# First tiles of a fused encoder block: small weights ahead of x, x's first tile in halves, some first weights through ScalarE's queue

## The chip, the cores and the metric

One NeuronCore of a Trainium2 chip. The metric is the device time of one execution in microseconds (us). A core has five engines that run beside each other: TensorE (PE in the rows; its weight loads are PEld), VectorE (DVE), ScalarE (ACT), GpSimd (POOL) and SyncE (SP), and 16 DMA engines that move data between the device's memory and the on-chip memory. SP, ACT and POOL can issue transfers.

## What is computed

One layer of a hybrid encoder trunk on x of 512 positions by 1024 channels, in float32. Cut to what stands at its start:

```
hn   = rms_norm(x, g_mix_pre)          # x * rsqrt(mean(x*x) + eps) * g
proj = hn @ w_in                       # 1024 -> 8192 columns
z_sgu, z_conv, z_pool, z_gate = split(proj)
br_b = conformer_conv(z_conv, ...) @ w_conv_out     # GLU, causal depthwise conv, layer norm, swish
...
h = x + rms_norm((gates * (br_a, br_b, br_c)).sum() @ w_out, g_mix_post)
h = h + rms_norm(swiglu(rms_norm(h, g_ffn_pre)), g_ffn_post)
out = h + sigmoid(h @ w_ple_gate) * (p @ w_ple)
```

## The kernel before, in words

Channels lie on the 128 partitions, the 512 positions along the free axis, so x is eight k-tiles of 128 channels by 512 positions. To keep float32 accuracy on TensorE, every operand is split into a high part (rounded) and a low part (the remainder), and each product is done three times: high by high, high by low, low by high (`mm3`, and `passes` in line 458). ScalarE makes a high part by a copy that rounds, VectorE the low part by a subtraction (`split`, line 177).

The order of the work at the start is written out by hand under `order()` (lines 459 to 518), which pins each instruction behind the one traced before it on its engine. The first products (`first_product`, lines 451 to 455) are six column blocks of 128 of the projection, the first three pairs of the conformer branch. They run with k outermost: for each k-tile of x, 3 passes by 6 blocks, 18 products of 128 by 512, into six accumulators (`banks`, line 449). x enters these products scaled by `g_mix_pre` alone; the factor of the norm, `x_inv`, comes later in `glu`. `x_high(k)` (line 388, ScalarE) scales and rounds a tile of x, `x_low(k)` (line 391, VectorE) makes its low part, `w_split(k)` (line 395) splits the 768 columns of weights of k-tile k. For k-tile 0 the weights come in two cuts (`first_cuts`, line 135): columns 0 to 255, blocks 0 and 1, whose high part VectorE makes (line 462), and columns 256 to 767, the other four blocks. Between, ScalarE squares x's tiles and VectorE sums the squares (`x_square`, `x_sums`); the two halves of the sums go through TensorE against a constant matrix (`channel_mean`, line 495, tile `ps_stat`), between the second and the third pass of k-tile 3.

The transfers are issued in lines 138 to 149: the vector of per-channel scales (`vec`) on ScalarE's queue, all else on SP's, in this order: x's tile 0, the two cuts of weights of k-tile 0, x's tile 1, the weights of k-tile 1, x's tiles 2 and 3, the weights of k-tile 2, x's tiles 4 to 7, the weights of k-tiles 3 to 7 (`X_AHEAD`, line 50, says how many tiles of x go ahead of each). A tile of x has 256 KB, a k-tile's weights 384 KB.

Before the data are there, TensorE runs a warm-up on zeros (lines 163 to 167): eight products of 512 columns and one of 256. VectorE fills the constant matrix and the zeros first; ScalarE makes a copy of one column (line 162), ahead of which stands the load of its activation table.

Of the kernel before, what the change touches and what calls it, by code (L numbers as in the profile page):

```python
# [8 lines left out]
F32 = mybir.dt.float32  # L9
F32R = mybir.dt.float32r  # L10
BF16 = mybir.dt.bfloat16
I32 = mybir.dt.int32
AF = mybir.ActivationFunctionType
# [3 lines left out]
P = 128  # L17
T = 512
H = 256
D = 1024  # L20
KT = D // P
NB = T // P
# [8 lines left out]
HALVES = (slice(0, H), slice(H, T))  # L31
FULL = slice(0, T)
# [8 lines left out]
N_RAW = 3  # L41
N_FIRST = 2 * N_RAW * P

N_WARM = 8

TAPS = (4, 3, 5, 3, 5)
TAPS_U = 4
# [2 lines left out]
X_AHEAD = (1, 2, 4, 8, 8, 8, 8, 8)  # L50

DMA_K = 5
STAT_K, STAT_A, STAT_H = 3, 1, 7

K_HALF = 4
# [36 lines left out]
def hybrid_block(  # L92
# [7 lines left out]
    nc = tc.nc  # L100
    order = InOrder(tc)
    dve, act_e = order.engine(nc.vector), order.engine(nc.scalar)
    pe_order = InOrder(tc)
    pe = pe_order.engine(order.engine(nc.tensor))

    const = ctx.enter_context(tc.tile_pool(name="const", bufs=1))
# [13 lines left out]
    def slot(tag, name, dt=F32R, shape=(2, T)):  # L120
        return act.tile([P, *shape], dt, tag=tag, name=name, bufs=6 if tag == "tm" else 8)
# [9 lines left out]
    x_all = wide_tile("x_all")  # L131
    first_all = wide.tile([P, KT * T], F32, tag="wide", name="first_all")
    first_raw = []

    def first_cuts(k):
        return ((0, 2 * P), (2 * P, N_FIRST)) if k == 0 else ((0, N_FIRST),)

    nc.scalar.dma_start(out=vec[:, :N_VEC], in_=vecs[:, :N_VEC])
    x_ahead = 0
    for k in range(KT):  # L140
        if k < 5:
            first_raw.append(first_all[:, k * N_FIRST:(k + 1) * N_FIRST])
        else:
            first_raw.append(slot("hn", "first_raw", F32, (D,))[:, :N_FIRST])
        while x_ahead < X_AHEAD[k]:
            nc.sync.dma_start(out=x_all[:, x_ahead], in_=xT[:, x_ahead])
            x_ahead += 1
        for c0, c1 in first_cuts(k):
            nc.sync.dma_start(out=first_raw[k][:, c0:c1], in_=w_first[k][:, c0:c1])

    def col(name, k):
        i = VECS.index(name) * KT + k
        return vec[:, i:i + 1]

    def tap(k, j):
        i = N_VEC + k * WIDTH + j
        return vec[:, i:i + 1]

    mean_mat = const.tile([P, P], F32R, name="mean_mat")
    dve.memset(mean_mat.bitcast(F32), 1.0 / D)  # L160
    warm = const.tile([P, 1], F32, name="warm")
    act_e.copy(warm, mean_mat.bitcast(F32)[:, :1])
    warm_up = const.tile([P, T], BF16, name="warm_up")
    dve.memset(warm_up, 0.0)
    ps = psum.tile([P, T], F32, tag="pst", name="ps_warm", bufs=1)
    for n in N_WARM * (T,) + (H,):
        pe.matmul(ps[:, :n], lhsT=warm_up[:, :P], rhs=warm_up[:, :n], start=True, stop=True)
    ident = const.tile([P, P], F32, name="ident")
    make_identity(nc, ident)
    cnt_i = const.tile([P, WINDOWS[-1]], I32, name="cnt_i")  # L170
# [61 lines left out]
    def blk(w, k):  # L232
        return w[:, k * P:(k + 1) * P]
# [144 lines left out]
    xg = [slot("br", f"xg{k}") for k in range(KT)]  # L378
    x_sums = row("x_sums")
    first = []  # L380
# [4 lines left out]
            pair = [stream.tile([P, D], F32R, tag=t, name=t) for t in ("hi", "lo")]  # L385
        first.append([w[:, :N_FIRST] for w in pair])

    def x_high(k):
        act_e.activation(out=xg[k][:, 0], in_=x_all[:, k], func=AF.Copy, scale=col("g_mix_pre", k))

    def x_low(k):
        dve.scalar_tensor_tensor(out=xg[k][:, 1], in0=x_all[:, k], scalar=col("g_mix_pre", k),
                                 in1=xg[k][:, 0], op0=ALU.mult, op1=ALU.subtract)
# [55 lines left out]
    banks = [bank("ps_first") for _ in range(2 * N_RAW)]  # L449

    def first_product(k, passes, js=range(2 * N_RAW)):
        for w, a in passes:
            for j in js:
                pe.matmul(banks[j], lhsT=blk(first[k][w], j), rhs=xg[k][:, a],
                          start=k == 0 and w == a == 0, stop=k == KT - 1 and w == 1)


    passes = ((0, 0), (0, 1), (1, 0))
    with order():
        (c0, c1), cut = first_cuts(0)  # L460
        hi, lo = (w[:, c0:c1] for w in first[0])
        dve.tensor_copy(hi, first_raw[0][:, c0:c1])
        x_high(0)
        dve.tensor_tensor(out=lo, in0=first_raw[0][:, c0:c1], in1=hi, op=ALU.subtract)
        x_low(0)
        hi, lo = (w[:, slice(*cut)] for w in first[0])
        split(hi, lo, first_raw[0][:, slice(*cut)])
        first_product(0, passes, range(c1 // P))
        first_product(0, passes, range(c1 // P, 2 * N_RAW))
        x_square(0)  # L470
        x_high(1)
        w_split(1)
        x_low(1)
        x_square(1)
        x_square(2)
        first_product(1, passes)
        x_high(2)
        w_split(2)
        x_low(2)
        for k in range(3, 6):  # L480
            x_square(k)
        first_product(2, passes)
        x_high(3)
        w_split(3)
        for k in range(6, KT):
            x_square(k)
        x_low(3)
        for k in (4, 5):
            x_high(k)
            w_split(k)  # L490
            if k == 4:
                x_halves = split_sums(x_sums)
            x_low(k)
        first_product(3, passes[:2])
        ps_x = channel_mean(x_sums, x_halves)
        first_product(3, passes[2:])
        for k in range(4, KT):
            if k >= 6:
                x_high(k)
                w_split(k)  # L500
        weights.ahead(2)
        weights.split = split
        rsqrt(x_inv, ps_x, t2("rs_t"))
        x_low(6)
        x_low(7)
        low = None
        for i in range(KT):
            t = t2("nrm")
            dve.scalar_tensor_tensor(out=t, in0=x_all[:, i], scalar=col("g_mix_pre", i),
                                     in1=x_inv, op0=ALU.mult, op1=ALU.mult)  # L510
            act_e.copy(hn[i][:, 0], t)
            if low:
                low()
            low = lambda i=i, t=t: dve.tensor_tensor(out=hn[i][:, 1], in0=t, in1=hn[i][:, 0],
                                                     op=ALU.subtract)
        low()
        for k in range(4, KT):
            first_product(k, passes)
# [3 lines left out]
    for k in range(N_RAW, KT):  # L522
        pair = []
        for _ in range(2):
            ps = bank("ps_ag")
            w = weights.get()
# [137 lines left out]
    for n in range(KT + SGU_LAG):  # L664
# [7 lines left out]
        else:  # L672
            i = n - SGU_LAG
            ps = branch_tile(sgu_T, TAPS[2])
# [38 lines left out]
    for g in GROUPS:  # L713
        for n in (2 * g, 2 * g + 1):
            ps = bank("ps_z")
# [9 lines left out]
    for n in range(KT + POOL_LAG):  # L725
# [6 lines left out]
        if n >= POOL_LAG:  # L732
            i = n - POOL_LAG
            ps = branch_tile(pool_T, TAPS[4])
# [30 lines left out]
    for n in range(KT):  # L765
        ps = branch_tile(conv_T, 0)
# [67 lines left out]
    with order():  # L834
# [6 lines left out]
        for i in range(N_HALF):  # L841
            n = KT - N_HALF + i
# [9 lines left out]
        for i in range(N_HALF):  # L852
            n = KT - N_HALF + i
# [11 lines left out]
        banks = [bank("ps_f") for _ in range(2 * N_PAIR)]  # L865
# [67 lines left out]
    for n in range(KT - 2):  # L933
        ps = bank("ps_fo")
# [31 lines left out]
    with order():  # L966
        ps, ps_last = bank("ps_fo"), bank("ps_fo")
        ffn_out(ps, KT - 2, 0, weights.get(2))
        ffn_out(ps_last, KT - 1, 0, weights.get(1))
        w = weights.get(1)  # L970
        ffn_out(ps, KT - 2, 1, w)
        weights.ahead(3)
        w = weights.get(2)
# [16 lines left out]
        for n in range(KT):  # L990
            hs = FULL if n < KT - 1 else HALVES[0]
            ps = ple_product(n, w_ple_1 if n >= 4 else w_ple_0, p_w, hs,
                             (lambda: inv_rms(f_sums, f_inv)) if n == PLE_STAT else None)
# [4 lines left out]
        banks = [bank("ps_pg") for _ in range(N_LAST)]  # L998
        for k, a in enumerate(h2):

            for w, x in ((0, 0), (1, 0), (0, 1)):
                for ps, block in zip(banks, blocks):
                    pe.matmul(ps, lhsT=blk(block[w], k), rhs=a[:, x],
                              start=k == w == x == 0, stop=k == KT - 1 and x == 1)
# [81 lines left out]
```

## Time and profile before

| | us |
|---|---|
| median of 3 runs | 973.61 (973.38 to 973.9) |
| the profiled execution | 974.28 |
| its span, first to last instruction | 972.5 |
| TensorE busy in it | 966.9 |
| VectorE, ScalarE busy | 673.3, 349.9 |

The profile shows one execution, instruction by instruction; times count from the first instruction. The profiled execution took 974.28 us, of which 972.5 are the span and 1.78 lie around it; it is 0.67 us slower than the median of the unprofiled runs. A DMA issue is a short instruction on the issuing engine's sequencer; its data land later.

### The profile page before, as it was taken

The numbers are of one execution on the slowest core, as the hardware profiler recorded it, in microseconds if no ns is written. First come the engines' busy times: TensorE is split into PE (matmuls) and PEld (weight loads), VectorE is DVE, ScalarE is ACT, GpSimd is POOL, SyncE is SP. The second block draws the span as 40 slices with busy tenths as digits, with TensorE's granted clock in tenths as the row PEclk, the third lists the DMA queues.
The fourth block names the chain that finished last, engine by engine and source line by source line (L and its number), as shares of the span: only waits on it lengthen the run. The fifth ranks groups of instructions, "written<-read, shape, count | busy, mean of one in ns | idle before, by whom it ended". The sixth has DMA issues, their size and how long they took to land.

```text
span 972.5 us, 11143 instructions
## 1 busy us (share of the span) xinstructions
PE 966.9 (99%) x4429; PEld 804.4 (83%) x4429; DVE 673.3 (69%) x868; ACT 349.9 (36%) x467; POOL 70.9 (7%) x51
## 2 busy tenths in 40 slices
PE   9999999999999999999999999999999999999998
PEld 6888888888888888888888988888888888888887
DVE  6997789999988899987555787544444442223684
ACT  7622333432224432156425353323232322223451
POOL 0100004000013712130000000000000000000000
PEclk9999999999999999999999999999999999999999
DMA  8832331322322332232337203222322333334311
GB/s 291 197 109 87 110 107 66 108 87 87 109 85 78 98 108 87 94 123 87 109 97 263 74 26 105 87 97 98 99 97 89 104 82 99 99 100 144 109 66 65
DMA packets 30724, 102.72 MB, mean 106 GB/s; under 512 B 3536, under 2 KB 4048, under 8 KB 30672
## 3 DMA queue, kind: packets, MB, share of 16 engines
q1 hardware_dynamic: 29808, 99.75, 31.0%
q0 software_dynamic: 720, 2.23, 1.3%
q8 instruction: 34, 0.56, 0.2%
q14 instruction: 18, 0.15, 0.0%
q10 hardware_dynamic: 144, 0.04, 0.0%
HBM read 97.68 MB, written 2.10 MB: 103 GB/s over the span
## 4 chain that ended last, share of the span: by engine, by line
PE 99%; DMA 1%; SPq 0%; DVE 0%; ACT 0%; issue 0%; DVEq 0%
PE ps_f L79 25%; PE ps_gate L79 13%; PE ps_br L79 13%; PE ps_fo L79 12%; PE ps_nat L79 9%; PE ps_ag L79 6%; PE ps_o L79 5%; PE ps_pg L79 5%; PE ps_z L79 4%; PE ps_first L79 3%; PE ps_ple L79 1%; PE ps_pool L79 1%; DMA first_all<-in_w_first 1%; PE ps_mix L79 1%; PE ps_stat L79 0%; PE ps_tr L79 0%
## 5 line engine op out<-in xcount | busy, mean ns | idle before, releaser
L79 ACT CAST hi<-raw 128x1024 fp32r<-128x1024 f32 (+2 forms) x160 | 165.2, 1033 | 459.4 <-PE ps_br L79 82.5
L79 DVE TENSOR_TENSOR lo<-raw,hi 128x1024 fp32r<-128x1024 f32 (+2 forms) x158 | 206.9, 1310 | 110.0 <-ACT hi L79 109.7
L79 DVE SCALAR_TENSOR_TENSOR acc<-h_conv,vec,acc 128x511 f32<-128x511 f32 (+14 forms) x240 | 183.1, 763 | 5.0
L79 PE MATMUL ps_f<-hg,hi 128*128 128x512 f32 (+1 forms) x608 | 183.3, 383 | 0.0
L79 PEld LDWEIGHTS ps_f<-hg,hi 128*128 128x128 f32 x608 | 113.1, 188 | 22.4
L79 PE MATMUL ps_gate<-hn,hi 128*128 128x512 f32 x384 | 119.0, 389 | 0.0
L79 PE MATMUL ps_f<-hg,lo 128*128 128x512 f32 (+1 forms) x304 | 116.4, 383 | 0.0
L79 PE MATMUL ps_fo<-f,hi 128*128 128x512 f32 x352 | 108.3, 389 | 0.0
L79 PEld LDWEIGHTS ps_gate<-hn,hi 128*128 128x128 f32 x384 | 72.0, 188 | 15.1
L79 PE MATMUL ps_nat<-hi,hn 128*128 128x512 f32 x256 | 78.8, 389 | 0.0
L79 PEld LDWEIGHTS ps_fo<-f,hi 128*128 128x128 f32 x352 | 66.1, 188 | 13.7
L79 PE MATMUL ps_gate<-hn,lo 128*128 128x512 f32 x192 | 74.8, 389 | 0.0
L79 PE MATMUL ps_fo<-f,lo 128*128 128x512 f32 x176 | 68.5, 389 | 0.0
L79 PEld LDWEIGHTS ps_f<-hg,lo 128*128 128x128 f32 x304 | 57.1, 188 | 11.3
L79 DVE TENSOR_TENSOR f<-ps_f,h_inv 128x512 f32<-128x512 f32 x22 | 15.2, 690 | 59.3 <-PE ps_f L79 59.3
L79 PEld LDWEIGHTS ps_nat<-hi,hn 128*128 128x128 f32 x256 | 48.0, 188 | 9.9
L79 PE MATMUL ps_nat<-lo,hn 128*128 128x512 f32 x128 | 49.8, 389 | 0.0
L79 PE MATMUL ps_ag<-hn,hi 128*128 128x512 f32 x160 | 49.2, 389 | 0.0
L79 PEld LDWEIGHTS ps_gate<-hn,lo 128*128 128x128 f32 x192 | 36.0, 188 | 7.5
L79 DVE TENSOR_TENSOR silu<-ps_f,h_inv 128x512 f32<-128x512 f32 x22 | 15.2, 690 | 36.7 <-PE ps_f L79 36.6
L79 PE MATMUL ps_br<-pool,hi 128*128 128x512 f32 x128 | 39.6, 389 | 0.0
L79 PE MATMUL ps_br<-sgu,hi 128*128 128x512 f32 x128 | 39.4, 389 | 0.0
(223 smaller groups left out, 1490.6 us busy)
## 6 DMA issues: line engine op xcount, KB each, us to landing
raw<-in_w_mix SPq DMA_DIRECT2D x90, 512.0 KB, 3.2
raw<-in_w_ffn_in SPq DMA_DIRECT2D x44, 512.0 KB, 3.2
raw<-in_w_ffn_out SPq DMA_DIRECT2D x16, 448.0 KB, 3.3
raw<-in_w_ffn_out SPq DMA_DIRECT2D x8, 512.0 KB, 3.5
raw<-in_w_ple_gate SPq DMA_DIRECT2D x8, 512.0 KB, 3.9
x_all<-in_xT SPq DMA_DIRECT2D x8, 256.0 KB, 7.2
h_all<-in_xT SPq DMA_DIRECT2D x4, 512.0 KB, 5.4
out_dram<-pg SPq DMA_DIRECT2D x7, 256.0 KB, 2.0
```

Source lines behind the costliest of these rows:

```text
L79: inst = op(*args, **kw)
```

## The change: order, size and queue of the first transfers, and the order of k-tile 0

- `N_WARM` goes from 8 to 7, and the warm-up's operand is a 128 by 128 tile, filled first, that is read four times over for the 512 columns.
- SP's first transfer is the first cut of k-tile 0's weights, then x's tile 0 in two halves of 256 positions. The second cut goes on ScalarE's queue, behind the vector.
- The weights of k-tile 1 (`K_ACT`) go on ScalarE's queue as well, pinned behind the copy of one column. All other transfers keep their queue and order.
- k-tile 0: x is scaled in halves; high and low weights of blocks 0 and 1 are multiplied with the high part of each half as it comes (eight half-width products), then the other four blocks' first pass, then the passes that are left.

```
+K_ACT = 1
-N_WARM = 8
+N_WARM = 7
...
+        cuts = first_cuts(k)
+        if k == 0:
+            c0, c1 = cuts[0]
+            nc.sync.dma_start(out=first_raw[0][:, c0:c1], in_=w_first[0][:, c0:c1])
+            cuts = cuts[1:]
+            for hs in HALVES:
+                nc.sync.dma_start(out=x_all[:, 0, hs], in_=xT[:, 0, hs])
+            x_ahead = 1
+            (c0, c1), cuts = cuts[0], ()
+            nc.scalar.dma_start(out=first_raw[0][:, c0:c1], in_=w_first[0][:, c0:c1])
         while x_ahead < X_AHEAD[k]:
             nc.sync.dma_start(out=x_all[:, x_ahead], in_=xT[:, x_ahead])
             x_ahead += 1
-        for c0, c1 in first_cuts(k):
-            nc.sync.dma_start(out=first_raw[k][:, c0:c1], in_=w_first[k][:, c0:c1])
+        if k != K_ACT:
+            for c0, c1 in cuts:
+                nc.sync.dma_start(out=first_raw[k][:, c0:c1], in_=w_first[k][:, c0:c1])
...
+    warm_up = const.tile([P, P], BF16, name="warm_up")
+    dve.memset(warm_up, 0.0)
     mean_mat = const.tile([P, P], F32R, name="mean_mat")
     dve.memset(mean_mat.bitcast(F32), 1.0 / D)
     warm = const.tile([P, 1], F32, name="warm")
-    act_e.copy(warm, mean_mat.bitcast(F32)[:, :1])
-    warm_up = const.tile([P, T], BF16, name="warm_up")
-    dve.memset(warm_up, 0.0)
+    with order():
+        act_e.copy(warm, mean_mat.bitcast(F32)[:, :1])
+        tc.keep_in_program_order(nc.scalar.dma_start(out=first_raw[K_ACT], in_=w_first[K_ACT]))
     ps = psum.tile([P, T], F32, tag="pst", name="ps_warm", bufs=1)
-    for n in N_WARM * (T,) + (H,):
-        pe.matmul(ps[:, :n], lhsT=warm_up[:, :P], rhs=warm_up[:, :n], start=True, stop=True)
+    ps = ps.rearrange("p (n c) -> p n c", n=NB)
+    for n in N_WARM * (NB,) + (NB // 2,):
+        pe.matmul(ps[:, :n], lhsT=warm_up, rhs=warm_up[:, None, :].broadcast_to([P, n, P]),
+                  start=True, stop=True)
...
-    def x_high(k):
-        act_e.activation(out=xg[k][:, 0], in_=x_all[:, k], func=AF.Copy, scale=col("g_mix_pre", k))
+    def x_high(k, hs=FULL):
+        act_e.activation(out=xg[k][:, 0, hs], in_=x_all[:, k, hs], func=AF.Copy,
+                         scale=col("g_mix_pre", k))
...
         dve.tensor_copy(hi, first_raw[0][:, c0:c1])
-        x_high(0)
         dve.tensor_tensor(out=lo, in0=first_raw[0][:, c0:c1], in1=hi, op=ALU.subtract)
+        for hs in HALVES:
+            x_high(0, hs)
+
+            for w in range(2):
+                for j in range(c1 // P):
+                    pe.matmul(banks[j][:, hs], lhsT=blk(first[0][w], j), rhs=xg[0][:, 0, hs],
+                              start=hs is HALVES[0] and w == 0, stop=False)
         x_low(0)
         hi, lo = (w[:, slice(*cut)] for w in first[0])
         split(hi, lo, first_raw[0][:, slice(*cut)])
-        first_product(0, passes, range(c1 // P))
-        first_product(0, passes, range(c1 // P, 2 * N_RAW))
+        rest = range(c1 // P, 2 * N_RAW)
+        first_product(0, passes[:1], rest)
+        first_product(0, passes[1:2], range(c1 // P))
+        first_product(0, passes[1:], rest)
```

## Rows read from the trace of the kernel before

**Rows 1.** The page: busy time of each engine (us, share of the span, instructions), and the shares of the engines in the chain that ended last.

```profile
PE 966.9 (99%) x4429; PEld 804.4 (83%) x4429; DVE 673.3 (69%) x868; ACT 349.9 (36%) x467; POOL 70.9 (7%) x51
...
PE 99%; DMA 1%; SPq 0%; DVE 0%; ACT 0%; issue 0%; DVEq 0%
```

**Rows 2.** The chain of work that ended last, first 42 us: start and length in us, what.

```profile
1.65 0.42 SPq L149
...
2.12 0.43 SPq L146
...
2.59 6.85 DMA first_all<-in_w_first
...
9.46 0.84 ACT first L79
...
10.35 11.49 PE ps_first L79 x48
```

**Rows 3.** The same chain over the whole span, two long pieces: 240 full products, 60 products of 256 columns.

```profile
40.01 54.40 PE ps_ag L79 x240
...
544.84 7.19 PE ps_o L79 x60
```

**Rows 4.** The timeline of the first 9 us, all engines: start, length, engine, line, instruction, out<-in and shapes, count, and in brackets the idle time before and what ended it.

```profile
0.74 0.40 ACTq L138 DMA_DIRECT2D vec<-in_vecs  x1
...
1.00 0.27 DVE L79 MEMSET warm_up<- 128x256 uint32 x1
...
1.17 1.28 ACT L79 ACT_TABLE_LOAD   x1 [1.17 <-PEq L1074]
...
1.33 3.81 PE L79 MATMUL ps_warm<-warm_up 128*128 128x512 bf16 x9 [1.33 <-DVE warm_up L79]
...
4.19 0.72 ACT L79 ACTIVATE xg<-x_all,vec 128x512 fp32r<-128x512 f32 x1 [1.53 <-DMA vec<-in_vecs]
...
4.55 4.24 SPq L146 DMA_DIRECT2D x_all<-in_xT  x4
...
4.96 4.81 PE L79 MATMUL ps_first<-xg,first 128*128 128x512 f32 x18
```

**Rows 5.** Two weight loads of the warm-up and the one at 12.00, from TensorE's timelines; and of the tile xg the row of its full products (duration ns min/median/max, first and last start).

```profile
2.16 0.15 PEld L79 LDWEIGHTS <-warm_up 128*128 128x128 bf16 x1 [0.28 <-issue]
2.59 0.15 PEld L79 LDWEIGHTS <-warm_up 128*128 128x128 bf16 x1 [0.28 <-issue]
...
12.00 2.15 PEld L79 LDWEIGHTS ps_first<-xg,first 128*128 128x128 f32 x10 [0.43 <-DVE xg L79]
...
L79 PE MATMUL ps_first<-xg,first x101: 387/389/797, 5.0 to 29.9; 128*128 128x512 f32 x101
```

**Rows 6.** Busy time in stretches of the start: stretch, length, then busy us and instructions of PE, PEld, DVE, ACT, POOL, then the granted clock, the busy share of the 16 DMA engines and GB/s.

```profile
4.00:6.00 2.00, 2.00 (x7) 0.83 (x6) 1.59 (x4) 1.74 (x3) 0.00 (x0) 1.00 0.74 212
6.00:8.00 2.00, 2.00 (x10) 1.68 (x10) 0.39 (x1) 0.14 (x1) 0.00 (x0) 1.00 0.91 298
8.00:10.00 2.00, 1.77 (x8) 1.13 (x6) 0.00 (x0) 1.26 (x2) 0.00 (x0) 1.00 1.02 387
10.00:12.00 2.00, 1.65 (x6) 1.05 (x6) 1.67 (x3) 2.00 (x5) 0.00 (x0) 1.00 1.05 405
```

**Rows 7.** Single transfers of the start, each from a stretch that holds its issue alone: out<-in, issuing queue, count, KB, us from issue to landing. In order: x's tile 0 (issued 0.74), the first cut of weights (1.18), the second (1.65), x's tile 1 (2.12), k-tile 1's weights (2.59), k-tile 3's weights (9.46).

```profile
x_all<-in_xT SPq DMA_DIRECT2D x1, 256.0 KB, 3.2
...
first_all<-in_w_first SPq DMA_DIRECT2D x1, 128.0 KB, 3.2
...
first_all<-in_w_first SPq DMA_DIRECT2D x1, 256.0 KB, 3.3
...
x_all<-in_xT SPq DMA_DIRECT2D x1, 256.0 KB, 6.3
...
first_all<-in_w_first SPq DMA_DIRECT2D x1, 384.0 KB, 6.8
...
first_all<-in_w_first SPq DMA_DIRECT2D x1, 384.0 KB, 6.0
```

**Rows 8.** A group of ScalarE's instructions by shape, from the second half of the kernel: the same operation as the scaling of x, on 256 columns: count, busy us, mean ns of one, idle before.

```profile
L79 ACT ACTIVATE hg<-h_all,vec 128x256 fp32r<-128x256 f32 x8 | 4.1, 511 | 9.5 <-DVE h_all L79 9.5
```

**Rows 9.** What SP's queue waited for in the first 20 us: us in total, times, longest.

```profile
SPq L146 <- DMA x_all<-in_xT: 1.8, 1, 1.8
SPq L149 <- DMA first_all<-in_w_first: 1.3, 2, 0.6
```

**Rows 10.** Timelines of ScalarE, VectorE and TensorE from 8.4 to 22 us.

```profile
8.47 0.73 ACT L79 ACTIVATE xg<-x_all,vec 128x512 fp32r<-128x512 f32 x1 [2.33 <-DMA x_all<-in_xT]
9.46 0.83 ACT L79 CAST first<-first_all 128x768 fp32r<-128x768 f32 x1 [0.26 <-DMA first_all<-in_w_first]
...
15.49 0.84 ACT L79 CAST first<-first_all 128x768 fp32r<-128x768 f32 x1 [0.60 <-DMA first_all<-in_w_first]
...
10.33 0.96 DVE L79 TENSOR_TENSOR first<-first_all,first 128x768 fp32r<-128x768 f32 x1 [3.93 <-ACT first L79]
...
16.99 0.95 DVE L79 TENSOR_TENSOR first<-first_all,first 128x768 fp32r<-128x768 f32 x1
...
20.79 0.69 DVE L79 TENSOR_TENSOR sum_half<-x_sums,sum_half 128x512 fp32r<-128x512 f32 x1
...
21.67 0.62 PE L79 MATMUL ps_stat<-sum_half,mean_mat 128*128 128x512 f32 x2
```

## The prediction

> **What bounds the kernel now.** I read the page first, for the engine that is never idle: TensorE is busy for 966.9 of 972.5 us and carries 99% of the chain that ended last [rows 1]. So an edit at the start is worth what it takes out of TensorE's first microseconds, provided that nothing later gives it back. Second the chain of waits over the first 42 us [rows 2]: the only link that isn't TensorE is the transfer of the second k-tile's weights. It was issued at 2.59, landed at 9.44, ScalarE rounded it by 10.30, and the products of k-tile 1 began at 10.35; from there TensorE runs through. Third, the pace: 54.40 us for 240 full products and 7.19 us for 60 products of half width [rows 3], that is 0.227 us and 0.120 us each, so a product cut in two costs 0.013 us more.
>
> Fourth the timeline of the start [rows 4]. The warm-up runs from 1.33 in steps of 0.427 us [rows 5], the pace of the 1.2 GHz level, and its last product touches the first real one at 4.96. That one waited for ScalarE's scaling of x's first tile, which ended at 4.91 (4.19 + 0.72) and itself began when the vector of scales had landed. The 18 products of k-tile 0 end at 9.77; the last is 0.389 us long as modelled [rows 5], so it was issued at 9.38 and a next one could have come at 9.61. At 0.227 us they would need 4.08 us and took 4.65: 0.57 us went to the low clock level at their start (the longest took 797 ns [rows 5]). Then come three losses that are waits: 0.74 us until 10.35 for ScalarE's rounding; 0.29 us at 12.00 for VectorE's low part of x (six products from 10.35 would have been through at 11.71); and some 0.16 us for the two restarts of the stream (the 48 products from 10.35 take 11.49 us less the last one's overhang of 0.16, against 10.88 at full pace: 0.45 us lost, the 0.29 among them). What can be won is therefore 0.74 + 0.45 = 1.19 us of waits plus what an earlier start gives.
>
> Fifth, the transfers [rows 6]. From 4 to 8 us the DMA engines are busy 74% and 91% of the time and move 212 and 298 GB/s; from 8 us on they move 387 to 405. Landings show it [rows 7]: x's first tile, the first weight block and the other blocks of k-tile 0 land 3.2 to 3.3 us after their issue, x's second tile 6.3, the weights of k-tile 1 6.8.
>
> **The change part by part.**
>
> *Small warm-up operand.* A 128-wide memset is now the first on VectorE (the 256-word one took 0.27 us, up to 1.27 [rows 4]). TensorE can start some 0.3 us earlier, at 1.0; 7.5 products at 0.427 us end at 4.2. Nothing else waits for them: they cost nothing while real work isn't ready, but leave TensorE idle from 4.2 to the first product, where there was no gap.
>
> *First tile in halves, small weights first.* The scaling of 256 columns takes 0.511 us [rows 8] where 512 took 0.72. If the scales still land just before 4.19 and x's first half by then, the first product can start at 4.19 + 0.51 = 4.70 plus the usual 0.05, at 4.75: 0.21 us earlier. ScalarE pays 2 x 0.511 - 0.72 = 0.30 us; its next step, rounding k-tile 0's other blocks, is needed only behind eight half-width products, so that hides; it would show only if those took under 1.2 us. Four products in halves cost 4 x 0.013 = 0.05 us. The low part of x waits for both halves, hence about 5.3 to 6.0, before TensorE asks for it. If x's first half lands late because it shares the engines with the blocks on ScalarE's queue, the start is lost: up to 0.6 us late at the worst (676 KB, the vector, x's first tile and its weights, had landed by 1.65 + 3.3 = 4.95 before). I take 4.75. The earlier start falls into the low clock level, where products advance at half pace, so the end of k-tile 0 moves less. The 0.57 us lost there are about one start and two slow products (0.17 + 2 x 0.2), so the level rose near 4.96 + 1.0 = 5.96 (the column of the granted clock says 1.00 in all of these stretches [rows 6]; the spacing of the products shows the lower level); with the same rise, some 2.4 products are done by then, 15.6 more at 0.227, plus 0.05, end at 9.55 for 9.61.
>
> *Three transfers to ScalarE's queue.* An issue there takes 0.40 us [rows 4]. The vector goes at 0.74, k-tile 0's other blocks behind it at 1.15; then the activation table (1.28 us) and the small copy, then the weights of k-tile 1: at 1.6 if the issue runs ahead of the table, at 3.1 if not; both before 4.19, when ScalarE has work. SP loses two issues of 0.4 us and gains one. That hides, since from the ninth transfer on its issues wait for landings [rows 9].
>
> *When does k-tile 1 land?* No row has two such queues loaded at once, so this is bounded. Ahead of its start stand the same 36 + 256 + 384 + 256 + 384 = 1316 KB as before, in another order. Upper bound: the same bytes at the same pace, so the last of x's second tile and its weights lands at 9.44. Lower: 676 KB by 4.95 as before, and the other 640 KB (655 kB) at the later 404 GB/s, 1.62 us, so 6.6. In between decides how much of the idle 9 to 26% of the DMA engines [rows 6] a second stream fills; I take the midpoint, T = 8.0, nearer to neither row. Behind T stand the scaling of x's second tile, 0.73, and the rounding of 768 columns, 0.83 [rows 10], if both land together: before, they were staggered, the first done before the second landed. TensorE's stream thus moves by (10.29 - 1.56) - T = 8.73 - T: 0.73 us earlier at 8.0, 0.71 later at 9.44, unchanged at 8.73.
>
> The Trainium skill ("DMA: Bandwidth & Descriptors", section "Issuing engines are not separate DMA queues") speaks against this: transfers issued from several engines run on the same 16 DMA engines and interleave, and only the issuing time is saved. By that rule the upper bound would hold and the sum would be +0.71 instead of -0.73 us.
>
> *What is late next.* The gain must pass VectorE, which from 10.33 on runs almost without a break [rows 10]. TensorE's statistics product at 21.67 needs the low half of the sums, ready at 20.79 + 0.69 = 21.48: 0.19 us of slack. VectorE's stream moves with k-tile 1, but only until it meets k-tile 3's weights: issued at 9.46, landing after 6.0 us [rows 7], rounded by 16.33, taken up at 16.99, so 0.66 us of slack. The cap is 0.85 us while those weights land at the same time; they stand behind the same bytes. The 0.73 fits under it. After 22 us all chains have moved together, and no other wait for an outside event is on TensorE's path.
>
> **Sum.** The profiled execution took 974.28 us, 972.5 of it span; 972.5 - 0.73 = 971.8. The median of the runs, 973.61, lies 0.67 below the profiled one; the same subtraction gives 972.9. About 0.2% (1.95 us) is what a measurement of this kernel can tell from no change; the forecast, and even all waits removed, lie inside it.
>
> **Rivals.**
>
> 1. *Same bytes, same pace*: x's second tile, now sharing the engines with its own weights, lands with them at 9.4, and ScalarE's two steps run behind both. For it: 212 GB/s at 4 to 6 us with issues enough in the queue, so more issues may not help. Against: idle shares of the DMA engines in that stretch. +0.7: 974.3. Chance 0.27. The section of the Trainium skill named above ("DMA: Bandwidth & Descriptors") states the rule that leads here.
> 2. *The old order again*: ScalarE issues the weights only at 3.1, behind its table load, and they stand behind x's second tile as before. Nothing moves: 973.6. Chance 0.10.
> 3. *The clock.* The new idle stretch before the first product keeps TensorE at 1.2 GHz for longer. Each product then costs 0.427 instead of 0.227 us. It decides once more than four further products are slow; with all 18 slow, k-tile 0 ends at 4.75 + 0.17 + 18 x 0.427 = 12.6 instead of 10.35, less some 0.4 us of waits that it covers: +1.9, 975.5. Against: the gap is half a microsecond. Chance 0.08.
> 4. *ScalarE's queue is held* (slower): from the ninth transfer on, an issue waits for an earlier landing (SP's waits [rows 9]; the issue of x's last tile ends at 8.79, behind the second tile's landing at 2.12 + 6.3). If the weights of k-tile 1 count among these, ScalarE stalls with everything queued behind it, and they land 6 us after an issue at 8.4: +5 to +6, 979. It decides when their landing passes 8.73. Against: program order puts them early. Chance 0.05.
>
> **How the numbers follow.** Forecast 0.50 at 972.9. Its own range reaches from T = 6.6, capped at 0.85 (972.7), or a little more if k-tile 3 lands earlier too, to T = 8.7; rivals 1 and 2 extend it to 974.3; with a quarter of a microsecond for the spread of the runs (973.38 to 973.9) on both sides: 972.2 to 974.6. Left out are rivals 3 and 4 and a tail, under 0.2. Faster by over 0.2% needs more than all the waits found: 0.03. Slower by over 0.2%: rival 4 and about a third of rival 3: 0.07. Within: 0.90.
>
> **What the profile after would show.** Right: the weights of k-tile 1 and x's second tile landed by about 8.0, products running through from 9.6 without a stop between k-tiles 0 and 1, and a small wait at the statistics product. Wrong: ScalarE's rounding of k-tile 1 ending after 10.29; weights landing first and x's second tile last; a first product after 5.0; full products still 0.427 us apart after 6 us; or an issue on ScalarE's queue later than 4 us.

## The result, and the profile after

The changed kernel took 976.83 us (median of 6 executions, 976.52 to 977.47) against 973.84 (973.38 to 974.17) for the kernel before on the same chip: a ratio of 1.003, 95% interval 1.002 to 1.0041. It is 3.0 us slower, where 0.7 us less was forecast. The profiled execution took 976.75 us, span 975.0. Several kernels below (e1, e2, e6, e10) have times in two groups some 2 us apart on one chip, and the one execution that was profiled is from the lower group each time.

Timeline of the kernel after, first 25 us (start, length, engine, line, instruction, out<-in, count, idle time before and what ended it):

```profile
0.99 3.38 PE L81 MATMUL ps_warm<-warm_up 128*128 128x512 bf16 x8 [0.99 <-DVE warm_up L81]
...
1.66 1.28 ACT L81 ACT_TABLE_LOAD   x1 [1.66 <-PEq L1100]
1.72 0.40 ACTq L179 DMA_DIRECT2D first_all<-in_w_first  x1
...
4.72 0.51 ACT L81 ACTIVATE xg<-x_all,vec 128x256 fp32r<-128x256 f32 x1 [1.58 <-DMA x_all<-in_xT]
...
5.28 0.74 PE L81 MATMUL ps_first<-xg,first 128*128 128x256 f32 x4 [0.91 <-ACT xg L81]
6.90 0.51 ACT L81 ACTIVATE xg<-x_all,vec 128x256 fp32r<-128x256 f32 x1 [1.67 <-DMA x_all<-in_xT]
...
7.46 2.97 PE L81 MATMUL ps_first<-xg,first 128*128 128x256 f32 x9 [1.44 <-ACT xg L81]
...
8.36 0.71 ACT L81 ACTIVATE xg<-x_all,vec 128x512 fp32r<-128x512 f32 x1
8.97 0.81 ACT L81 CAST first<-first_all 128x768 fp32r<-128x768 f32 x1
...
23.79 0.62 PE L81 MATMUL ps_stat<-sum_half,mean_mat 128*128 128x512 f32 x2
```

TensorE now stops twice, each time for ScalarE's scaling of a half of x's first tile: 0.91 us until 5.28, and 1.44 us until 7.46. Where before it took 4.96 to 9.77 for k-tile 0 [rows 4], its first eight half-width products alone last until about 8 us. ScalarE is no longer waiting when k-tile 1's data come (8.36 and 8.97 have no idle time in front). The statistics product stands at 23.79 instead of 21.67 [rows 10].

The chain that ended last (start, length, what) shows which transfer TensorE waited for, the second half of x's first tile, where before it was k-tile 1's weights [rows 2]:

```profile
1.65 5.23 DMA x_all<-in_xT
6.88 0.02 issue
6.90 0.52 ACT xg L81
7.42 0.04 issue
7.46 16.49 PE ps_first L81 x66
```

What the two queues moved from 3 to 6 us, while that half was under way (queue: packets, MB, share of the 16 engines; q10 is ScalarE's queue, with 0.69 MB in the whole execution, the 676 KB that ScalarE issues; q1 is SP's):

```profile
q10 hardware_dynamic: 269, 0.61, 56.6%
q1 hardware_dynamic: 247, 0.27, 34.0%
```

From 7.46 on the 66 products run in one piece, so k-tile 1 is not waited for. But they run slowly at first. Busy time in stretches, with the columns of [rows 6] (granted clock, DMA share and GB/s last):

```profile
4.00:6.00 2.00, 1.09 (x6) 0.54 (x4) 0.00 (x0) 0.51 (x1) 0.00 (x0) 1.00 0.94 303
6.00:8.00 2.00, 0.56 (x5) 0.54 (x5) 0.56 (x1) 1.10 (x3) 0.00 (x0) 1.00 1.05 403
8.00:10.00 2.00, 2.00 (x7) 1.63 (x6) 0.98 (x3) 2.00 (x4) 0.00 (x0) 0.51 1.04 405
10.00:12.00 2.00, 2.00 (x8) 1.55 (x7) 2.00 (x3) 2.00 (x4) 0.00 (x0) 0.63 1.06 394
```

TensorE was busy 1.09 and 0.56 of 2 us from 4 to 8 us; then the granted clock falls to 0.5, the 1.2 GHz level, from 8.06 to 11.47. Ahead of that it stood at the 2.4 GHz level: the half-width products start 0.119 us apart, much as the 0.120 of [rows 3]. In the low stretch products start 0.427 us apart, later 0.23. Eight are slow, some 0.2 us each: 1.6 us.

The mean granted clock of every execution is on record. A stretch like this one takes about 0.002 off it. It is 0.997 or 0.998 in four of the six executions of the changed kernel, and 0.999 or 1.0 in all 99 executions of the kernel before that ran beside the experiments. The two slowest (977.05 and 977.47) have 1.0; that TensorE was at the low level in them too, ahead of the first clock record (see e5), is argued and not shown.

The end of the program moved too. The last product starts at 968.52 before and 970.62 after, 2.10 later, but the spans differ by 2.46: the time behind it grew from 3.99 to 4.35 us. What SP's queue waited for in the last microseconds, before and after:

```profile
SPq L1081 <- DMA out_dram<-pg: 1.0, 1, 1.0
```

```profile
SPq L1107 <- DMA out_dram<-pg: 1.4, 1, 1.4
```

The baseline was read too slow as well. A second profiled execution of the kernel before (e0 below) has a span of 971.9: k-tile 1's weights land at 8.85, not 9.44, and the statistics product stands at 21.07. Against that one, which is near the median, the change costs 2.72 us at the statistics product and 0.36 at the end, 3.08 in all; the medians differ by 2.99.

### The profile page after: what moved, and what is told of

Its sections match the earlier page's. It is cut to its first block, busy times and chain, and to the rows that moved or that the text cites. A ratio compares the mean times of both kernels' runs of the same rounds, so it can differ in the third digit from the quotient of the medians.

```text
span 975.0 us, 11154 instructions
## 1 busy us (share of the span) xinstructions
PE 967.6 (99%) x4432; PEld 805.7 (83%) x4432; DVE 673.7 (69%) x868; ACT 348.8 (36%) x468; POOL 70.9 (7%) x51
## 4 chain that ended last, share of the span: by engine, by line
PE 99%; DMA 1%; DVE 0%; SPq 0%; ACT 0%; issue 0%; DVEq 0%
PE ps_f L81 25%; PE ps_gate L81 13%; PE ps_br L81 13%; PE ps_fo L81 12%; PE ps_nat L81 9%; PE ps_ag L81 6%; PE ps_o L81 5%; PE ps_pg L81 4%; PE ps_z L81 4%; PE ps_first L81 4%; PE ps_ple L81 1%; PE ps_pool L81 1%; PE ps_mix L81 1%; DMA x_all<-in_xT 1%; PE ps_stat L81 0%; PE ps_tr L81 0%
## 5 line engine op out<-in xcount | busy, mean ns | idle before, releaser
L81 PE MATMUL ps_br<-conv,hi 128*128 128x512 f32 x128 | 39.4, 389 | 0.0
```

Source lines behind the costliest of these rows:

```text
L81: inst = op(*args, **kw)
```

## The experiments

**Theories.** (Z) The weights on ScalarE's queue take DMA engines from x's second half; TensorE stops for it, and the idle time brings the low clock. (Y) The low clock comes from the shorter warm-up and the gap before the first product, whatever the queues. (X) The new order of k-tile 0's products costs the time. Below, "after" is the changed kernel; landings are from each run's one trace.

**e3_one_queue**: after, second cut and k-tile 1's weights back on SP's queue; order, halves and warm-up stay.

```
-            nc.scalar.dma_start(out=first_raw[0][:, c0:c1], in_=w_first[0][:, c0:c1])
+            nc.sync.dma_start(out=first_raw[0][:, c0:c1], in_=w_first[0][:, c0:c1])
...
-        if k != K_ACT:
+        if True:
...
-        tc.keep_in_program_order(nc.scalar.dma_start(out=first_raw[K_ACT], in_=w_first[K_ACT]))
```

> The changed kernel with both transfers back on SP's queue: small weights, x's halves, second cut, x's tile 1, weights of k-tile 1, all in one line. Theory A: x's second half lands by 4.3, no gap of over 0.5 us inside k-tile 0, no low clock after 6 us; k-tile 1's weights land at about 9.4 again, so the time is the old one, 973.3 to 974.3. Theories B and C: 976 to 977.

973.55 us (973.42 to 974.02, 11 executions), ratio 0.9998 (0.9989 to 1.0007). All of the loss is gone, so X falls: the order and the halves stayed. The short warm-up stayed too, but here it reaches the first product, so Y is not tested by this run. The timeline (columns as above):

```profile
3.54 0.51 ACT L81 ACTIVATE xg<-x_all,vec 128x256 fp32r<-128x256 f32 x1 [0.88 <-DMA x_all<-in_xT]
...
4.11 6.14 PE L81 MATMUL ps_first<-xg,first 128*128 128x256 f32 x24
...
4.91 0.51 ACT L81 ACTIVATE xg<-x_all,vec 128x256 fp32r<-128x256 f32 x1 [0.86 <-DMA x_all<-in_xT]
...
7.75 0.84 ACT L81 CAST first<-first_all 128x768 fp32r<-128x768 f32 x1 [0.25 <-DMA first_all<-in_w_first]
```

x's halves land at 3.46 and 4.89 instead of 4.63 and 6.88, though the same transfers are issued at 1.18 and 1.65. From 3 to 6 us SP's queue has the DMA engines to itself:

```profile
q1 hardware_dynamic: 445, 0.72, 94.4%
```

And k-tile 1's weights land at 7.73, x's second tile at 6.75: in this trace one queue brings k-tile 1 about as early as two did (7.66). It is one trace; e12, with all weights on SP's queue as well, has 8.21.

**e1_w1_on_sp**: after, only k-tile 1's weights back on SP (the last two hunks of e3).

> The changed kernel with the weights of k-tile 1 back on SP's queue, in their old place behind x's second tile; the other blocks of k-tile 0 stay on ScalarE's queue. Theory A (the transfers on ScalarE's queue hold up x's second half, and the idle TensorE then falls to 1.2 GHz): with 256 KB instead of 640 KB on ScalarE's queue, x's second half lands by about 5.0 instead of 6.88, the first 18 products never show the 0.427 us spacing after 7 us, and the time is that of the kernel before, 973.3 to 974.5. Theory B (the new order on SP, small weights ahead of a halved x, is what costs, whatever the queue): as slow as the changed kernel, about 976.8. Theory C (the shorter warm-up costs): also about 976.8.

973.71 us, ratio 1.0007 (0.9998 to 1.0016): six times of 973.3 to 973.7 and five of 975.0 to 975.9. x's second half lands at 5.43, the first product starts at 5.40 after 1.2 us of waiting, products of the second half follow without a stop, and the profiled execution (973.66) shows no low clock behind it.

**e2_cut_on_sp**: after, only the second cut back on SP (e3's first hunk).

> The changed kernel with the second cut of k-tile 0's weights back on SP's queue, behind x's two halves; the weights of k-tile 1 stay on ScalarE's queue. Theory A: 384 KB issued at about 1.2 share the DMA engines with x's halves, so x's second half lands at 5.5 to 6.5, between the two, and the second cut later still; 974.5 to 976.5, and if TensorE's clock falls, near the upper end. Theories B and C: 976.8.

975.99 us, ratio 1.0018 (1.0009 to 1.0027): four times of 973.9 to 974.2, seven of 975.5 to 977. x's second half lands at 5.71, k-tile 1's weights at 5.38, the first product starts at 5.51. So either transfer on the second queue adds an idle start, and the two together cost most. That x's second half is late is shown for both together and, in this one trace, for k-tile 1's weights; for the cut alone it is not, since e9 and e11 below, with e1's first transfers, have it at 4.72 and 5.06, against 4.89 in e3. There it is the first half that comes later, 4.07 to 4.75 against 3.46. The weights of k-tile 1 are the greater part: without them 2.2 us of the loss go by the ratios, without the cut 1.2. These ratios mix the two groups: the lower ones are near 973.5 (e1) and 974.0 (e2), close to before's 973.71 on this chip, and how many executions fall in the upper one, five of 11 and seven of 11, makes up most of the difference.

**e4_gaps_filled**: after, with a longer warm-up and six products on zeros between the halves, so that TensorE hardly idles.

```
-N_WARM = 7
+N_WARM = 10
+N_FILL = 6
...
+            if hs is HALVES[0]:
+                for _ in range(N_FILL):
+                    pe.matmul(ps_warm, lhsT=warm_up, rhs=warm_up[:, None, :].broadcast_to([P, NB, P]),
+                              start=True, stop=True)
```

> The changed kernel with its transfers untouched, but TensorE is kept busy with zeros: three more warm-up products and six products on zeros between the two halves of k-tile 0 (work that the reference does not need). Theory A: x's second half lands at 6.9 as before the edit, but the clock no longer falls between 8 and 11.5; the eight or so products at 0.427 us come back at 0.227, 1.6 us: 975.0 to 975.4. What then remains over 973.8 is the wait for x's second half. If the clock cost nothing and the wait all: 976.8 or more.

975.06 us (974.87 to 976.05), ratio 1.0016 (1.0008 to 1.0025). The transfers land as in after (x's second half at 6.74), but the clock stays at 1.0:

```profile
5.45 0.74 PE L82 MATMUL ps_first<-xg,first 128*128 128x256 f32 x4 [0.51 <-ACT xg L82]
6.03 1.47 PE L82 MATMUL ps_warm<-warm_up 128*128 128x512 bf16 x6
7.32 4.90 PE L82 MATMUL ps_first<-xg,first 128*128 128x256 f32 x22
```

This takes the low clock away on nearly the same late data (x's second half 0.14 us earlier): 976.83 - 975.06 = 1.77 us (on two chips whose medians of before differ by 0.13), which fits the eight slow products, 1.6, and the 0.14. The other 1.3 us is the late half and the end of the program. No execution of e4 has a mean clock under 0.999; its three longest times (975.82 to 976.05) have spans of 973.1 and 973.2 like the rest, so what makes them longer lies outside the span.

**e5_short_warmup**: the kernel before with the small, shorter warm-up alone.

```
-N_WARM = 8
+N_WARM = 7
...
+    warm_up = const.tile([P, P], BF16, name="warm_up")
+    dve.memset(warm_up, 0.0)
...
+    for n in N_WARM * (NB,) + (NB // 2,):
+        pe.matmul(ps[:, :n], lhsT=warm_up, rhs=warm_up[:, None, :].broadcast_to([P, n, P]),
...
```

> The kernel before with the changed kernel's warm-up alone (small operand, filled first, 7 products and a half). The warm-up ends at about 4.2 and the first product stays near 4.9, so TensorE is idle for some 0.7 us. Theory A (late halves and their gaps): 973.3 to 974.2, in one group. Theory C (the warm-up is too short, and the clock falls for it): a group of runs at 975 or more, median 975 to 976.

974.6 us (973.81 to 974.99), ratio 1.0005 (0.9996 to 1.0014). The time lies between what the two theories expected. The first product waits until 5.09 and products stay 0.427 us apart until 8.9. Windows, columns as above:

```profile
6.00:8.00 2.00, 2.00 (x6) 1.39 (x6) 0.29 (x1) 0.94 (x2) 0.00 (x0) 1.00 0.89 306
```

Six products against ten in [rows 6], at a clock column that says 1.00 in both: at the start the column does not show the level, the spacing does. The first clock record of this trace stands at 8.90, where the spacing changes; in before and e0 it stands at 5.94 and 6.13, and there too the spacing changes. So the low level of the warm-up lasted some 3 us longer. Y is right on the mechanism; by the ratio it is worth about half a microsecond here, and the interval includes 1.

**e9_long_warmup**: e1 with `N_WARM` 10 for 7, so that the warm-up reaches the first product.

> The run with k-tile 1's weights on SP (second cut on ScalarE's queue), whose times fell into two groups, 973.3 to 973.7 and 975.0 to 975.9, with three warm-up products more, so that TensorE is busy from 1.0 to the first product at about 5.3. If the idle 1.2 us ahead of the first product is what lets the clock fall in the slow group: one group, 973.0 to 973.9. If the groups come from the landing of the transfers: two groups again.

973.47 us (973.3 to 974.02), ratio 0.9996 (0.9988 to 1.0005). The upper group of e1 is gone. Timeline of TensorE:

```profile
0.99 4.11 PE L81 MATMUL ps_warm<-warm_up 128*128 128x512 bf16 x11 [0.99 <-DVE warm_up L81]
4.86 15.63 PE L81 MATMUL ps_first<-xg,first 128*128 128x256 f32 x70
20.33 0.62 PE L81 MATMUL ps_stat<-sum_half,mean_mat 128*128 128x512 f32 x2
```

The statistics product stands 0.74 us ahead of e0's, as much as was forecast, with k-tile 1's weights on SP. But in e13 below, whose first transfers are those of before, it stands at 20.80, so by that trace the lead is 0.47. The end of the program takes back 0.36 of it.

**e10_after_long_warmup**: after, with `N_WARM` 10 and nothing else.

> The changed kernel with three more warm-up products (TensorE busy until the first product at 5.3) and nothing else, so that of its two idle stretches only the second, ahead of x's second half, is left. If the low clock after 8 us needs both stretches: as with both filled, 974.9 to 975.5. If the second alone (1.4 us) is enough: 976.4 to 977, or two groups of runs, one at each.

975.16 us (8 executions), ratio 1.002 (1.001 to 1.0031): five times of 974.6 to 975.3, three of 976.75 to 976.9. The second stop stays (1.3 us of waiting until 7.38). The profiled execution, one of the lower group, has no low clock behind the stop. The upper three lie where all of after's times lie, and their mean granted clock is 0.998, against 0.999 or 1.0 in the other five: the clock fell in these three. So the second stop alone is enough, in some executions.

**e8_w1_later**: after, with k-tile 1's weights issued on ScalarE's queue behind the two scalings.

```
-        tc.keep_in_program_order(nc.scalar.dma_start(out=first_raw[K_ACT], in_=w_first[K_ACT]))
...
+            if hs is HALVES[1]:
+                tc.keep_in_program_order(nc.scalar.dma_start(out=first_raw[K_ACT], in_=w_first[K_ACT]))
```

> The changed kernel with k-tile 1's weights still on ScalarE's queue, but issued behind the scaling of both halves of x's first tile instead of at 1.7. Theory A: x's second half lands at 5.4 as in the run with these weights on SP; the weights are issued near 6 and land at 8 to 9; the time is 973.3 to 974.3 when the clock holds. As TensorE is idle from 4.2 to 5.4 here too, some runs may be in a slow group at 975 to 976. If the halves cost by themselves, all runs are at 976.

977.19 us (976.77 to 978.51, 5 executions), ratio 1.0035 (1.0021 to 1.0049): a miss. x's second half lands at 4.79, as Z says, but the weights, issued at 4.82, land 6.3 us later, at 11.16. From 5 to 7 us none of their packets moves, though nothing else stands on ScalarE's queue; nearly all move from 8 to 11, behind what SP had queued by 4.8. What TensorE waited for (total, times, longest), and the stretches around it:

```profile
PE ps_first L81 <- ACT first L81: 2.5, 1, 2.5
```

```profile
10.00:12.00 2.00, 0.00 (x0) 0.00 (x0) 0.00 (x0) 0.81 (x2) 0.00 (x0) 1.00 1.05 404
12.00:14.00 2.00, 1.93 (x5) 1.58 (x6) 1.95 (x3) 2.00 (x5) 0.00 (x0) 0.61 1.03 411
```

A stop of 2.5 us, and again the low clock behind it (12.44 to 15.85), with the DMA engines full all the time: the same exchange, paid by the other transfer.

**e6_w1_on_act_alone**: the kernel before, only k-tile 1's weights moved to ScalarE's queue.

```
-        for c0, c1 in first_cuts(k):
+        for c0, c1 in first_cuts(k) if k != 1 else ():
...
+        tc.keep_in_program_order(nc.scalar.dma_start(out=first_raw[1], in_=w_first[1]))
```

> The kernel before with one part of the change alone: the weights of k-tile 1 on ScalarE's queue behind the small copy (issued at about 1.3), x's first tile still whole and first on SP's queue, the old long warm-up. Theory A (what stands on ScalarE's queue takes the DMA engines from what SP queues at the same time): those weights land at about 7 instead of 8.9, and x's first tile, the two cuts and x's second tile later than before (x at 4.5 to 5.5, second cut at 6 to 6.5); one restarts earlier, the other later, 973.5 to 975. If a second queue simply adds rate: 972.9 to 973.5, everything landing earlier.

973.9 us, ratio 1.0009 (1.0 to 1.0018): seven times of 973.6 to 973.9, four of 975.6 to 975.7. The weights land at 5.52, some three microseconds earlier than before, and nothing is gained: the first cut lands at 5.16, so the first product waits until 5.62, and x's second tile, at 7.87, is now the later of the two.

**e12_half_on_act**: e3 with x's second half on ScalarE's queue, `N_WARM` 8.

```
-            for hs in HALVES:
-                nc.sync.dma_start(out=x_all[:, 0, hs], in_=xT[:, 0, hs])
+            for hs, queue in zip(HALVES, (nc.sync, nc.scalar)):
+                queue.dma_start(out=x_all[:, 0, hs], in_=xT[:, 0, hs])
```

> A version meant to beat both: all weights on SP's queue in the new order, only x's second half (128 KB) on ScalarE's queue, so that both halves travel beside the first weights and nothing large does; one more warm-up product. Theory A: both halves land by 4.3, products run from about 4.9 without a gap of over 0.3 us inside k-tile 0, no low clock after 6.5; 972.9 to 973.6 in one group. If the order of the new transfers still costs something by itself: above 974.

973.65 us, ratio 1.0004 (0.9995 to 1.0013). The halves land at 4.24 and 4.43; the second cut now lands at 6.32 and TensorE waits for its rounding until 7.01. No gain; one execution of 11 took 976.13, with a mean clock of 0.998.

**e0_before_again**: the kernel before, unchanged, for a second trace.

> The kernel before once more, for a second trace. If the slow transfers from 4 to 8 us (212 and 298 GB/s, k-tile 1's weights landing at 9.44) belong to its order of transfers, they come again, and its products of k-tile 1 start at 10.2 to 10.5. If they belonged to that one execution (which was the slowest but one of its runs), the weights land by about 7.7, as they do in the one-queue run, and the products of k-tile 1 start before 9.9.

973.64 us, span 971.9. Products of k-tile 1 start at 10.10, 0.06 us late, and the wait for x's low part costs 0.16: far less than the 0.74 and 0.29 read from the first trace. So the outcome lies between the two that were expected. Also in e13 and e5, with the same transfers, k-tile 1's weights land at 8.57 and 9.06.

**e13_one_more_dma**: the kernel before, with a transfer that nothing needs at the start cut in two. **e11_merged**: e9 with x's last two tiles in one transfer, which brings the count of transfers back to that of before. The first code cut is e13's, the second e11's.

```
-    nc.sync.dma_start(out=vec[:, N_VEC:], in_=vecs[:, N_VEC:])
+    N_MID = N_VEC + WIDTH * KT // 2
+    nc.sync.dma_start(out=vec[:, N_VEC:N_MID], in_=vecs[:, N_VEC:N_MID])
+    nc.sync.dma_start(out=vec[:, N_MID:], in_=vecs[:, N_MID:])
```

```
-            nc.sync.dma_start(out=x_all[:, x_ahead], in_=xT[:, x_ahead])
-            x_ahead += 1
+            n = 2 if x_ahead == KT - 2 else 1
+            nc.sync.dma_start(out=x_all[:, x_ahead:x_ahead + n], in_=xT[:, x_ahead:x_ahead + n])
+            x_ahead += n
```

> The kernel before with one more transfer in all: the load of the convolution's taps, which nothing waits for in its first 30 us, is issued as two. In the traces of all kernels with the halves (one transfer more than before) the span ends 4.35 us after the last product's start, in those without 3.99. Theory D: the end of the program waits for the eight landing counters one after another, and the last output's transfer sits on the last counter before and on the first one with a transfer more, so that seven more waits of some 0.06 us follow its landing. Then this kernel's span ends 4.35 us after its last product's start, and its time is 0.3 to 0.4 us longer than before's, 973.9 to 974.3. If the tail belongs to something else in the change: 3.99, and no difference.

> A version meant to beat both: the run with the long warm-up and k-tile 1's weights on SP (973.5 against 973.9), with x's tiles 6 and 7 in one transfer, so that the count of transfers is that of before. Theory D: its span ends 3.99 us after the last product's start instead of 4.35; 0.36 us less, 973.0 to 973.3, and 0.4 to 0.7 us under the kernel before. Otherwise 973.5. The two tiles land together near 13.8 and aren't needed before 15.

e13: 974.17 us, ratio 1.0007 (0.9998 to 1.0016), and 4.36 us from the start of the last product to the end of the span. e11: 973.47 us, ratio 0.9996 (0.9987 to 1.0005), and 3.99 us; the span came out as expected, the time not. The times can't tell 0.36 us apart, the traces do. SP's instructions on semaphores at the program's end (count, duration, first and last start), in before, then e13, then e11:

```profile
L1081 SPq EVENT_SEMAPHORE  x10: 17/28/28, 970.2 to 972.4; - x10
```

```profile
L1083 SPq EVENT_SEMAPHORE  x10: 17/28/28, 970.6 to 971.9; - x10
```

```profile
L1107 SPq EVENT_SEMAPHORE  x10: 17/28/28, 969.4 to 971.7; - x10
```

Ten each time. With the count of before, their starts spread over 2.2 and 2.3 us: most are through before the last output has landed. With one transfer more it is 1.3: they all begin behind it. The semaphores that the instructions carry in the traces show why. SP waits in turn, in these traces always in the same order, for eight semaphores on which its transfers count their landings. In before, e0 and e11 the last output counts on the last of the eight, and seven waits are through before it lands; in after and e13 it counts on the first, and the seven others, 0.06 us apart, follow its landing. One transfer more moved the last output from the last semaphore to the first, and the end by 0.36 us.

## Why the prediction was wrong

1. **"If x's first half lands late ... up to 0.6 us late at the worst", first product at 4.75.** This is the step that failed. For the first product the bound held, at 5.28, 0.53 us late. But the 676 KB that it counted, the vector, the whole tile and its own weights, left out the 384 KB of k-tile 1, which the same part of the prediction puts on the other queue at 1.6, right beside x; and no stop between the halves was priced. x's second half landed at 6.88, not by 4.95 (6.74 in e4 and 6.79 in e10, with the same transfers); where k-tile 1's weights are behind it on SP, it landed at 5.43 (e1), 4.72 (e9), 5.06 (e11) and 4.89 (e3). Its products started at 7.46. Up to the statistics product, against e0: a start 0.16 us later, a stop of 1.6 us between the halves and some 0.35 us for half-width products and small delays, less 1.0 us that e0 lost to slow first products and to its waits, make 1.1 of the 2.72 us. The other 1.6 are the low clock.
2. **The clock.** Rival 3 named idle time and the low clock and had 0.08. The ground for its low chance, a gap of half a microsecond, fell with step 1: there were two, together over 2 us of waiting. But it had the low level last on from the warm-up through all of k-tile 0, as e5 shows it for nine products; in after's trace the first products ran at the full pace and the clock fell later, for eight products. That its price, 1.9, is near the 1.77 that e4 measured is therefore luck.
3. **T = 8.0.** Right: x's second tile landed at 7.66, the weights at 7.07, and ScalarE's rounding ended at 9.78, ahead of 10.29. Whether the second queue is the reason stays open, since one queue did as well in one trace (e3, 7.73) and not in another (e12, 8.21). Part of the gain was no gain, since the baseline's 9.44 was a late landing (e0, 8.85). The rule of the Trainium skill that was weighed ("DMA: Bandwidth & Descriptors", "Issuing engines are not separate DMA queues") said that transfers of several engines interleave on the same DMA engines. The trace agrees in what that costs, x's half at 6.88; the upper bound that the prediction set beside it, 9.44, was not reached in any other trace, on one queue or two, but for e8's, where these weights are issued at 4.82.
4. **"What can be won is therefore 0.74 + 0.45 = 1.19 us of waits".** Too high, from one profiled execution that was 0.67 us over the median; e0's two waits are 0.06 and 0.16 us. In the order of before the statistics product stands at 21.67, 21.07 (e0) and 20.80 (e13), so a lead of 0.7 us over one trace, like that of e9 over e0, is about what two traces of the same start differ by.
5. **The end.** Nothing was priced for one transfer more; it cost 0.36 us.
6. **Rivals 1, 2 and 4 did not come.** Of rival 1 only the order came, the weights first and x's second tile last, but at 7.66. ScalarE issued the weights at 1.72, beside its table load (the timeline above), and its issues were held nowhere.

The sum, against a median of 973.84: 1.77 for the clock, 0.36 for the end, and the 0.9 that is left for the late half less what k-tile 1 gave back: 3.0. The last term is a remainder; by the two traces of point 1 the terms are 1.6, 0.36 and 1.1. Of the five signs of being wrong that were named beforehand three came: the weights landing before x's second tile, a first product after 5.0, and products 0.427 us apart after 6 us. The first of them was no fault here, since both landed in time.

No kernel here is shown to beat the one before: e9 and e11 have the lowest medians, both with a ratio of 0.9996 and 1 inside the interval.

## What to carry to other kernels

In this kernel a second issuing queue did not bring the first-needed data earlier: x's first half landed at 3.46 with one queue (e3) and at 4.07 to 4.86 with two. What is issued early on the second queue is served ahead of or beside what the other holds, so bound a transfer's landing by all bytes issued up to it, and together with it, on every queue, and for its last piece, not its first. TensorE, started on late data, paid twice here, in waiting and then in a lower clock, so a warm-up should last until the first product has its data, with margin for landings that differ by more than half a microsecond between executions. And a wait is counted as winnable only when a second profile of the same kernel shows it.

## What the runs showed of the hardware that was not expected

- Landings of the same transfers differ by 0.7 us and more between executions: in the order of before (before, e0, e13, e5) k-tile 1's weights landed at 9.44, 8.85, 8.57 and 9.06, and the second cut of k-tile 0's at 4.96, 5.15, 5.89 and 7.04; x's second half in e1 and e9, with the same transfers ahead, at 5.43 and 4.72.
- Over both queues together, the first 15 to 18 transfers of SP and ScalarE behind the vector landed in the order in which they were issued, in all 15 traces. The only pairs out of order were issued within 0.01 us of each other, but for one in e8 (issued at 4.56 and 4.82, landed at 11.35 and 11.16). So the two queues behave here like one line in order of issue, in which neighbours share the DMA engines.
- ScalarE's queue issued a transfer at 1.72 while the load of its activation table ran from 1.66 to 2.94.
- A transfer issued on an otherwise empty queue at 4.82 landed 6.3 us later (e8), about as one on the full queue did (6.8 in [rows 7]).
- One transfer more in the whole program moved its end by 0.36 us.
